# Two hybrid decoder layers in fp32r: the float32 work between the weights' matmuls put together at fewer points

## The chip, the cores and the metric

The kernel runs on one core of one Trainium2 chip. The metric is the device time of one execution in microseconds (us). The kernel before took 1279.74 us (median of three runs, 1278.59 to 1279.90).

## The reference, cut to what matters

Two layers over 256 tokens of width 1024. Each is a half-step SwiGLU, a layer norm, three token mixers on one input projection (a gated DeltaNet, a sliding-window attention with sinks, a cross-attention to 256 memory rows), a gated merge with one output projection, a layer norm, a second SwiGLU, a layer norm:

```python
def hybrid_layer(x, mem_n, ...):
    h = layer_norm(ALPHA * x + 0.5 * swiglu(x, ffn1_w_gu, ffn1_w_down), ln_g[0], ln_b[0])
    (dn_q, dn_k, dn_v, dn_b, dn_a, dn_z, sw_q, sw_k, sw_v, xa_q, gates) = split(h @ w_in)
    o_dn = deltanet_branch(dn_q, dn_k, dn_v, dn_b, dn_a, dn_z, ...)
    o_sw = sliding_window_attention(sw_q, sw_k, sw_v, swa_sinks)
    o_xa = memory_cross_attention(xa_q, mem_n, w_mem_kv)
    merged = sum(sigmoid(gates) * einsum('bsnc,ncd->bsnd', stack(o_dn, o_sw, o_xa), w_branch))
    h = layer_norm(ALPHA * h + merged @ w_out, ln_g[1], ln_b[1])
    return layer_norm(ALPHA * h + 0.5 * swiglu(h, ffn2_w_gu, ffn2_w_down), ln_g[2], ln_b[2])
```

All inputs and outputs are float32.

## The kernel before, in words

Every weight is streamed once, as 512 KB units of 128 rows by 1024 (`unit`, line 115 for its DMA). A unit is split into a rounded part `whi` (a cast on ScalarE) and the rest `wlo` (a subtraction on VectorE), both at line 121 in `split`. A product with weights is three fp32r matmuls (`mm3`, line 130: high by high, high by low, low by high). Activations that meet weights are split in the same way, into two halves of a tile such as `hT`. All other products (transposes at line 133, attention values, the DeltaNet's chunk products) are plain float32 matmuls. In the trace a float32 product of 128 columns is two rows, a transpose one.

In the mixers the order of TensorE's instructions is kept as written (`pinned`); elsewhere a scheduler orders them. `weave(work, steps)` runs the matmuls of the gates (`gates(n)`, eight steps of 12 matmuls, in two column halves of four units each) and of the branch outputs (`branch(n)`, four steps of 12), and calls the small float32 pieces after the step whose number stands in its table:

- `x_turn(tb)` transposes the cross-attention's probabilities of one block of 128 tokens (eight transposes into two PSUM tiles; ScalarE copies one out, VectorE the other). `x_values(tb)` multiplies them with the values and splits the result.
- `w_turn(0, hh)` is the same for the window attention: four transposes, one copy on ScalarE. `w_scores` and `w_values` are its scores and its values.
- `rec_v0`, `rec_s1`, `rec_r1`, `rec_v1`, `rec_qs`, `rec_o0`, `rec_o1` are the DeltaNet's recurrence over two chunks, eight matmul rows each through `heads`. `rec_r1` ends in four VectorE instructions at line 935 that make `R1`, and `rec_v1` reads `R1`. `rec_o0` is the first chunk's output; `finish` norms it, `finish_turn` transposes it.

The small pieces take their PSUM from two pools of two banks each: `at` and `sm`.

A projection that ends in a norm (`projA` with `ends`) computes token block 0, then block 1 in three column pieces: 512 columns into `acc`, and two of 256 into `at`. `Post.__call__` norms block 0 meanwhile and leaves two closures in `turns`; each is `to_T`, which transposes 512 normed columns into an `sm` bank and splits them into `hT` (a cast on ScalarE, a subtraction on VectorE). They run between the pieces of block 1. Behind the projection stands `Ffn.first`: for each token block 16 matmuls with the high half of `hT` (lines 323 and 324) and eight with its low half (line 326).

Of the kernel before, what the change touches and what calls it, by code (L numbers as in the profile page):

```python
# [38 lines left out]
def tile_trunk(ctx, tc, x, xT, mem, memT_, wst, lnp, memln, cvw, rows, cst, out):  # L39
# [30 lines left out]
    def at():  # L70
        return T(psT, [P, 512], "at")

    def sm():
        return T(psS, [P, 512], "sm")
# [54 lines left out]
    def matmul(*a, **k):  # L129
        return pe(nc.tensor.matmul(*a, **k))  # L130

    def transpose(*a):
        return pe(nc.tensor.transpose(*a))  # L133
# [43 lines left out]
    def projA(xt, w, kpu, nk, outs, tail=0, dsts=(), lead=0, after=None, behind=None, held=(), led=None, along=None, ends=()):  # L177

        def one(k, kk, hi, lo, tb, j):
            ts = slice(tb * P, (tb + 1) * P)  # L180
            n = [o.shape[-1] for o in outs[tb]]
            first = k == ((nu - tail) * kpu if tb and j and ends and len(outs[1]) > 2 else 0)
            c = kk * w + sum(n[:j])
            c = slice(c, c + n[j])
            mm3(outs[tb][j], (xt[0](k)[:, ts], xt[1](k)[:, ts]), (hi[:, c], lo[:, c]), first, k == nk - 1 or bool(ends and tb and j and k == (nu - tail) * kpu - 1))

        nu = nk // kpu
        units = {}

        def get(uu):  # L190
            if uu not in units:
                t = uu - (nu - tail)
                units[uu] = unit(kpu * w, dsts[t] if 0 <= t < len(dsts) else None, behind=behind if uu in held else None)
            return units[uu]

        def run(us, tb, js):
            for uu in us:
                for kk in range(kpu):
                    for j in js:
                        one(uu * kpu + kk, kk, *get(uu), tb, j)  # L200

        for tb in range(2):
            run(range(lead), tb, range(len(outs[tb])))
            if led:
                led(tb)
        for uu in range(lead, nu - tail):
            for tb in range(2):
                run([uu], tb, range(len(outs[tb])))
            if along and uu in along:
                along[uu](*newest)  # L210
        for uu in range(nu - tail, nu):
            get(uu)
        turns = ()
        if ends:
            after.early(outs[1].pop())
            outs[1] += ends
        for tb in range(2):
            for j in range(len(outs[tb])):
                run(range(nu - tail, nu), tb, [j])
                if j and turns:  # L220
                    turns.pop(0)()
            turns = after and after(tb, outs)

    def full_rows():
# [289 lines left out]
    def mixers(l, hT, mkT, mv_, post):  # L514
# [180 lines left out]
        def x_turn(tb):  # L695
            pT = prs[2 + tb] = T(p2, [P, 2, 4, P], "pt")
            for kb in range(2):
                ps = at().rearrange("p (h k) -> p h k", h=4)
                for h in range(4):
                    transpose(ps[:, h, :], prs[tb][:, h, kb * P:(kb + 1) * P], ident)  # L700
                (nc.vector.tensor_copy if kb else nc.scalar.copy)(pT[:, kb], ps)

        def x_values(tb):
            if not oX:
                oX.extend(T(pu, [P, 4, S], tag, F32R) for tag in ("u6", "u7"))
            ts = slice(tb * P, (tb + 1) * P)
            ps = at().rearrange("p (h k) -> p h k", h=4)
            for h in range(4):
                for kb in range(2):
                    matmul(ps[:, h, :], mv_[:, kb, h * P:(h + 1) * P], prs[2 + tb][:, kb, h, :], start=kb == 0, stop=kb == 1)  # L710
            split(oX[0][:, :, ts], oX[1][:, :, ts], ps)
# [36 lines left out]
        def w_turn(tb, hh):  # L748
            if hh == 0:
                wpT[tb] = [T(p2, [P, 2, 4, P], "pt") for _ in range(tb + 1)]  # L750
            for kb in range(tb + 1):
                ps = at().rearrange("p (h k) -> p h k", h=4)
                for h in range(4):
                    transpose(ps[:, h, :], wpr[tb, hh][:, h, kb * P:(kb + 1) * P], ident)

                (nc.vector.tensor_copy if kb else nc.scalar.copy)(wpT[tb][kb][:, :, 2 * hh:2 * hh + 2, :].rearrange("p v i q -> p i v q"), ps.rearrange("p (i v) q -> p i v q", v=2))
# [218 lines left out]
        def branch(n, o):  # L975
# [16 lines left out]

        weave(gates(0), {
            1: [lambda: x_scores(1), lambda: products(1, 0), lambda: products(1, 1), inverses],
            3: [lambda: x_turn(0)],
            4: [lambda: x_values(0)],
            5: [lambda: x_turn(1)],
            6: [lambda: x_values(1)],
            7: [lambda: w_scores(0, 0)],
            8: [lambda: w_scores(0, 1)]})  # L1000
        weave(branch(0, oX), {
            2: [lambda: w_turn(0, 0)],
            3: [lambda: w_turn(0, 1), begin_inverse],
            4: [lambda: w_scores(1, 0)]})
        weave(gates(1), {
            1: [lambda: w_values(0), double],
# [9 lines left out]
            3: [rec_s1],  # L1016
            4: [rec_r1]})
        weave(gates(2), {
            1: [rec_o0],
            2: [rec_v1, rec_qs],  # L1020
            3: [rec_o1],
            5: [lambda: finish_turn(0)],
            8: [lambda: finish_turn(1)]})
# [31 lines left out]
    ps = sm()  # L1055
# [125 lines left out]
```

## Time and profile before

| | |
|---|---|
| runs | 1278.59, 1279.74, 1279.90 us |
| profiled execution | 1280.75 us, span 1279.0 us |
| TensorE matmul | 1263.0 us busy, 99% |
| weight loads | 1073.8 us, 84% |
| VectorE | 866.5 us, 68% |
| ScalarE | 660.6 us, 52% |
| GpSimd | 210.6 us, 16% |
| chain that ended last | 89% TensorE, 4% DMA, 3% VectorE |

TensorE is called PE in the rows, its weight load PEld, VectorE DVE, ScalarE ACT, GpSimd POOL. Matmuls overlap in the pipeline, so the time that a matmul costs is the distance from its start to the next start, not its duration.

### The profile page before, as it was taken

What the parts mean: (1) busy time and instruction counts of PE and PEld (TensorE: products, weight loads), DVE (VectorE), ACT (ScalarE), POOL (GpSimd) and SP (SyncE); (2) the same over time, 40 slices, a digit from 0 to 9 for tenths busy, and PEclk for the clock granted to TensorE, in tenths of its full rate; (3) what the DMA queues carried; (4) which work ended last, traced back from release to release, by engine and by line L of the source; (5) the groups of instructions that cost most, each with busy time, mean ns of one, the idle gap of its engine ahead of it and who ended that gap; (6) DMA issues with size and microseconds to landing.
All of it is one profiled execution on the core that took longest, in us unless ns stands there. A gap on an engine that the chain in (4) does not pass through costs nothing.

```text
span 1279.0 us, 18765 instructions
## 1 busy us (share of the span) xinstructions
PE 1263.0 (99%) x6948; PEld 1073.8 (84%) x6948; DVE 866.5 (68%) x1271; ACT 660.6 (52%) x980; POOL 210.6 (16%) x365
## 2 busy tenths in 40 slices
PE   9999999999999999999999999999999999999997
PEld 6888889999878788888888888899987787888886
DVE  5788576886647776665776665759767388766655
ACT  6556444655664534444354554456656654444441
POOL 0232100002311202221012220010033102122200
PEclk9999999999999999999999999999999999999999
DMA  8988764655534728776667876556463256577762
GB/s 285 315 269 278 254 210 161 206 176 129 170 116 148 259 97 265 244 239 220 224 204 243 256 253 223 173 187 209 152 163 136 97 191 221 167 246 244 237 225 82
DMA packets 77499, 261.40 MB, mean 204 GB/s; under 512 B 11904, under 2 KB 13056, under 8 KB 77408
## 3 DMA queue, kind: packets, MB, share of 16 engines
q1 hardware_dynamic: 66320, 232.53, 55.2%
q0 software_dynamic: 11088, 27.68, 8.0%
q8 instruction: 54, 0.88, 0.3%
q14 instruction: 37, 0.30, 0.1%
HBM read 246.40 MB, written 13.76 MB: 203 GB/s over the span
## 4 chain that ended last, share of the span: by engine, by line
PE 89%; DMA 4%; DVE 3%; issue 2%; POOL 1%; ACT 1%; SPq 0%; DVEq 0%; ACTq 0%; POOLq 0%
PE acc L130 79%; PE at L130 3%; PE sm L130 3%; DMA raw<-in_wst_dram 2%; DVE wlo L121 2%; PE sm L133 1%; DMA w<-dr 1%; PE acc L323 1%; PE acc L324 1%; PE acc L326 1%; ACT whi L121 1%; PE at L133 1%; POOL t L797 1%; POOL l L788 0%; POOL t L798 0%
## 5 line engine op out<-in xcount | busy, mean ns | idle before, releaser
L121 DVE TENSOR_TENSOR wlo<-raw,whi 128x1024 fp32r<-128x1024 f32 (+2 forms) x403 | 489.3, 1222 | 282.1 <-ACT whi L121 280.2
L121 ACT CAST whi<-raw 128x1024 fp32r<-128x1024 f32 (+2 forms) x403 | 413.4, 1033 | 401.8 <-PE acc L130 321.4
L130 PE MATMUL acc<-whi,hT 128*128 128x512 f32 (+1 forms) x1824 | 563.2, 386 | 0.7 <-ACT whi L121 0.6
L130 PEld LDWEIGHTS acc<-whi,hT 128*128 128x128 f32 x1824 | 340.5, 188 | 70.3 <-ACT whi L121 3.0
L130 PE MATMUL acc<-wlo,hT 128*128 128x512 f32 (+1 forms) x912 | 350.7, 385 | 0.8 <-DVE wlo L121 0.8
L130 PE MATMUL acc<-whi,u 128*128 128x512 f32 x784 | 249.0, 392 | 0.0
L130 PEld LDWEIGHTS acc<-wlo,hT 128*128 128x128 f32 x912 | 171.6, 188 | 33.8 <-DVE wlo L121 1.7
L130 PEld LDWEIGHTS acc<-whi,u 128*128 128x128 f32 x784 | 147.3, 188 | 30.6
L130 PE MATMUL acc<-wlo,u 128*128 128x512 f32 x392 | 152.8, 390 | 0.0
L353 POOL DMA_DIRECT2D tr<-t x176 | 96.2, 553 | 304.3 <-DVE t L347 295.1
L130 PE MATMUL acc<-hT,whi 128*128 128x256 f32 x672 | 122.3, 284 | 0.0
L130 PEld LDWEIGHTS acc<-hT,whi 128*128 128x128 f32 x672 | 104.7, 192 | 0.0
L130 PE MATMUL acc<-hT,wlo 128*128 128x256 f32 x336 | 95.2, 283 | 0.0
L130 PEld LDWEIGHTS acc<-wlo,u 128*128 128x128 f32 x392 | 73.7, 188 | 14.7
L130 PEld LDWEIGHTS acc<-hT,wlo 128*128 128x128 f32 x336 | 64.4, 192 | 0.0
L354 POOL DMA_DIRECT2D pt<-tr x44 | 25.0, 568 | 194.7 <-DMA tr<-t 148.5
L344 ACT ACTIVATE t<-acc 128x256 f32<-128x256 f32 x88 | 33.5, 380 | 38.3 <-PE acc L130 38.2
L990 POOL TENSOR_TENSOR u<-u,gt 128x512 f32<-128x512 f32 x16 | 24.4, 1529 | 131.0 <-DVE gt L988 131.0
L345 DVE TENSOR_TENSOR t<-t,acc 128x256 f32<-128x256 f32 x88 | 36.7, 417 | 9.1 <-ACT t L344 4.7
L121 DVE TENSOR_TENSOR u<-pt,u 128x512 fp32r<-128x512 f32 x44 | 28.9, 657 | 11.8 <-ACT u L121 11.8
L121 DVE TENSOR_TENSOR u<-raw,u 128x1024 fp32r<-128x1024 f32 x24 | 30.9, 1290 | 7.4 <-ACT u L121 7.4
L130 PE MATMUL acc<-whi,w 128*128 128x512 f32 x96 | 31.8, 402 | 3.6 <-DVE w L121 3.5
(236 smaller groups left out, 1204.3 us busy)
## 6 DMA issues: line engine op xcount, KB each, us to landing
raw<-in_wst_dram SPq DMA_DIRECT2D x409, 512.0 KB, 4.4
tr<-t POOLq DMA_DIRECT2D x176, 64.0 KB, 3.8
pt<-tr POOLq DMA_DIRECT2D x44, 256.0 KB, 5.0
raw<-in_wst_dram SPq DMA_DIRECT2D x16, 324.0 KB, 2.9
gB<-in_lnp_dram SPq DMA_DIRECT2D x6, 512.0 KB, 5.9
bB<-in_lnp_dram SPq DMA_DIRECT2D x6, 512.0 KB, 5.9
w<-dr POOLq DMA_DIRECT2D x4, 512.0 KB, 11.5
t<-in_xT_dram SPq DMA_DIRECT2D x4, 256.0 KB, 6.1
```

Source lines behind the costliest of these rows:

```text
L121: return nc.scalar.copy(hi, src).ins, nc.vector.tensor_tensor(lo, src, hi.bitcast(F32), op=ALU.subtract).ins
L130: return pe(nc.tensor.matmul(*a, **k))
L133: return pe(nc.tensor.transpose(*a))
L323: nc.tensor.matmul(ps, hT[0][:, k, ts], hi[:, c], start=k == 0, stop=False)
L324: nc.tensor.matmul(ps, hT[0][:, k, ts], lo[:, c], start=False, stop=False)
L326: nc.tensor.matmul(ps, hT[1][:, k, ts], hi[:, c], start=False, stop=k == KD - 1)
L344: act = nc.scalar.activation(t[:, :, tb, :], g, AF.Silu).ins
L345: ins = nc.vector.tensor_tensor(t[:, :, tb, :], t[:, :, tb, :], u, op=ALU.mult).ins
L353: nc.gpsimd.dma_start(d[:, :, q].rearrange("b c x -> c b x"), z[32 * q:32 * q + 32].rearrange("c (b x) -> c b x", b=4))
L354: back = nc.gpsimd.dma_start(y, d.rearrange("b c q x -> (b c) (q x)")).ins
L797: nc.gpsimd.tensor_tensor(pr16[:, :, 0:n], ab[j // 8][:, j % 8, :, j + 1:16], y16[:, :, j:j + 1].to_broadcast([P, 8, n]), op=ALU.mult)
L990: nc.gpsimd.tensor_tensor(mg[tb][:, js], mg[tb][:, js], gt[tb][:, js], op=ALU.add)
```

## The change: what it does

In the mixers, `x_turn(0)` and `x_turn(1)` run together after step 4 of the first gates (before: steps 3 and 5), and `x_values(0)` and `x_values(1)` after step 6 (before: 4 and 6). As four PSUM tiles are then wanted at once, block 1 takes its two from `sm` in place of `at`. `w_turn(0, 0)` joins `w_turn(0, 1)` after step 3 of the first branch. `rec_o0` moves from step 1 of the third gates behind `rec_v1` and `rec_qs` after step 2. In `projA` both closures of `turns` run after block 1's last piece (before: one after each 256-column piece).

```diff
             for j in range(len(outs[tb])):
                 run(range(nu - tail, nu), tb, [j])
-                if j and turns:
-                    turns.pop(0)()
+                if j == 2:
+                    for f in turns:
+                        f()
...
-                ps = at().rearrange("p (h k) -> p h k", h=4)
+                ps = (sm if tb else at)().rearrange("p (h k) -> p h k", h=4)
...
-            3: [lambda: x_turn(0)],
-            4: [lambda: x_values(0)],
-            5: [lambda: x_turn(1)],
-            6: [lambda: x_values(1)],
+            4: [lambda: x_turn(0), lambda: x_turn(1)],
+            6: [lambda: x_values(0), lambda: x_values(1)],
...
-            2: [lambda: w_turn(0, 0)],
-            3: [lambda: w_turn(0, 1), begin_inverse],
+            3: [lambda: w_turn(0, 0), lambda: w_turn(0, 1), begin_inverse],
...
         weave(gates(2), {
-            1: [rec_o0],
-            2: [rec_v1, rec_qs],
+            2: [rec_v1, rec_qs, rec_o0],
             3: [rec_o1],
```

TensorE's order at the third gates of layer 0, before, from `rec_r1` to the first matmuls behind `rec_qs`. `sm_3931` is `rec_r1`, `sm_3963` is `rec_o0`, `sm_4008` is `rec_v1`, `sm_4015` is `rec_qs`; the `acc` rows are weights.

```order
L130 MATMUL sm_3931<-w_462_2587,u_385_2070 128x128 x4
...
L130 MATMUL acc_3943<-whi_3945,hT_1598 128x512
L130 MATMUL sm_3963<-w_461_2586,u_463_2588 128x128 x4
L130 MATMUL acc_3942<-whi_3991,hT_1598 128x512
...
L130 MATMUL acc_3943<-whi_3991,hT_1598 128x512
L130 MATMUL sm_4008<-w_462_2587,w_471_2598 128x128 x4
L130 MATMUL sm_4015<-w_462_2587,u_386_2071 128x128 x4
L130 MATMUL acc_3942<-whi_4022,hT_1598 128x512
```

The same place now; `sm_3980` is `rec_v1`, `sm_3987` is `rec_qs`, `sm_3994` is `rec_o0`.

```order
L130 MATMUL sm_3931<-w_462_2587,u_385_2070 128x128 x4
...
L130 MATMUL acc_3943<-whi_3945,hT_1598 128x512
L130 MATMUL acc_3942<-whi_3963,hT_1598 128x512
...
L130 MATMUL acc_3943<-whi_3963,hT_1598 128x512
L130 MATMUL sm_3980<-w_462_2587,w_471_2598 128x128 x4
L130 MATMUL sm_3987<-w_462_2587,u_386_2071 128x128 x4
L130 MATMUL sm_3994<-w_461_2586,u_463_2588 128x128 x4
L130 MATMUL acc_3942<-whi_4022,hT_1598 128x512
```

Between `rec_r1` and `rec_v1` there is one float32 group fewer; it stands behind `rec_qs` now.

ScalarE's order at layer 0's last norm, before. The `hT` rows are the casts of the transposed blocks: `sm_5966` and `sm_5991` are block 0's first and second 512 columns, `sm_6017` and `sm_6026` are block 1's; the `whi` rows are weights of the next SwiGLU.

```order
L279 ACTIVATE rstd_5919<-bnmv_5917,epsc 128x1
L121 CAST hT_5911<-sm_5966 128x4x128
L121 CAST whi_6052<-raw_6051 128x1024
L121 CAST whi_6124<-raw_6123 128x1024
L121 CAST hT_5911<-sm_5991 128x4x128
L279 ACTIVATE rstd_6008<-bnmv_6006,epsc 128x1
L121 CAST hT_5911<-sm_6017 128x4x128
```

The same place now (`sm_5984` is block 0's first 512 columns):

```order
L280 ACTIVATE rstd_5919<-bnmv_5917,epsc 128x1
L121 CAST whi_6052<-raw_6051 128x1024
L121 CAST whi_6124<-raw_6123 128x1024
L121 CAST hT_5911<-sm_5984 128x4x128
L121 CAST hT_5911<-sm_5991 128x4x128
L280 ACTIVATE rstd_6008<-bnmv_6006,epsc 128x1
L121 CAST hT_5911<-sm_6017 128x4x128
```

Block 0's first cast stands behind the two casts of weights now, not ahead of them.

TensorE's order at layer 0's second norm, as the difference of the two (`sm_4470`, now `sm_4488`, is block 0's first 512 columns, `sm_4495` its second; the `at` rows are block 1's last two pieces).

```order
 L130 MATMUL at_4284<-u_788_4367,w_754_4250 128x256
-L133 MATMUL sm_4470<-cs,h_218 128x128 x4
 L130 MATMUL at_4285<-u_773_4337,w_751_4247 128x256
...
 L130 MATMUL at_4285<-u_788_4367,w_754_4250 128x256
+L133 MATMUL sm_4488<-cs,h_218 128x128 x4
 L133 MATMUL sm_4495<-cs,h_218 128x128 x4
```

The first four transposes stand behind the last piece's 18 matmuls now, directly ahead of `Ffn.first`. The same holds in layer 1's second norm and in layer 0's last. At the two first norms, and where the last norm writes the output, the order of TensorE is as it was.

## Rows read from the trace of the kernel before

**Rows 1.** The page's first part: busy time and share of each engine.
```profile
PE 1263.0 (99%) x6948; PEld 1073.8 (84%) x6948; DVE 866.5 (68%) x1271; ACT 660.6 (52%) x980; POOL 210.6 (16%) x365
```

**Rows 2.** PE's longest total wait: who, for whom, us in all, times, longest.
```profile
PE acc L130 <- DVE w L121: 3.5, 4, 1.1
```

**Rows 3.** Timeline of PE around float32 groups: start us, us, instruction, count.
```profile
304.75 0.39 PE L130 MATMUL acc<-whi,hT 128*128 128x512 f32 x1
...
307.48 1.03 PE L133 MATMUL at<-cs,pp 128*128 128x128 f32 x8
...
311.11 1.95 PE L130 MATMUL at<-pt,u 128*128 128x128 f32 x16
...
315.63 1.03 PE L133 MATMUL at<-cs,pp 128*128 128x128 f32 x8
...
333.37 0.60 PE L133 MATMUL at<-cs,pp 128*128 128x128 f32 x4
...
336.56 0.60 PE L133 MATMUL at<-cs,pp 128*128 128x128 f32 x4
```

**Rows 4.** Timeline of layer 0's recurrence, `rec_r1` to `rec_qs`.
```profile
390.75 1.05 PE L130 MATMUL sm<-w,u 128*128 128x128 f32 x8
...
394.37 1.05 PE L130 MATMUL sm<-w,u 128*128 128x128 f32 x8
...
397.60 0.60 DVE L935 SCALAR_TENSOR_TENSOR w<-sm,neg,u 128x128 f32<-128x128 f32 x2
...
397.79 0.39 PE L130 MATMUL acc<-whi,hT 128*128 128x512 f32 x1
...
398.34 1.13 PE L130 MATMUL sm<-w,w 128*128 128x128 f32 x8 [0.16 <-DVE w L935]
...
399.51 0.58 ACT L942 COPY w<-sm 128x512 f32<-128x512 f32 x1 [0.24 <-PE sm L130]
...
400.12 0.48 PE L130 MATMUL acc<-whi,hT 128*128 128x512 f32 x1
```

**Rows 5.** The same `rec_v1` in layer 1.
```profile
1030.84 1.13 PE L130 MATMUL sm<-w,w 128*128 128x128 f32 x8 [0.16 <-DVE w L935]
```

**Rows 6.** Timeline of PE and ACT at layer 0's last norm.
```profile
638.40 0.40 PE L130 MATMUL at<-whi,u 128*128 128x256 f32 x2
...
638.76 2.00 ACT L121 CAST whi<-raw 128x1024 fp32r<-128x1024 f32 x2 [1.23 <-PE at L130]
...
639.23 0.48 PE L323 MATMUL acc<-whi,hT 128*128 128x512 f32 x1
...
640.67 0.58 ACT L121 CAST hT<-sm 128x512 fp32r<-128x512 f32 x1
...
641.30 0.50 PE L323 MATMUL acc<-whi,hT 128*128 128x512 f32 x1
```

**Rows 7.** Timeline of PE, ACT and DVE at layer 0's second norm.
```profile
454.55 0.60 PE L133 MATMUL sm<-cs,h 128*128 128x128 f32 x4
...
457.46 0.48 PE L323 MATMUL acc<-whi,hT 128*128 128x512 f32 x1
...
457.74 0.58 ACT L121 CAST hT<-sm 128x512 fp32r<-128x512 f32 x1 [1.97 <-PE sm L133]
...
458.40 0.64 DVE L121 TENSOR_TENSOR hT<-sm,hT 128x512 fp32r<-128x512 f32 x1
...
460.86 1.42 DVE L287 SCALAR_TENSOR_TENSOR h<-h,rstd,bB 128x512 f32<-128x512 f32 x2
...
461.76 0.63 PE L133 MATMUL sm<-cs,h 128*128 128x128 f32 x4
```

**Rows 8.** Timeline around the window's transposes and its first values.
```profile
337.19 0.59 ACT L756 COPY pt<-at 128x512 f32<-128x512 f32 x1 [1.23 <-PE at L133]
337.88 3.90 ACT L121 CAST whi<-raw 128x1024 fp32r<-128x1024 f32 x4
...
344.25 1.08 PE L130 MATMUL at<-pt,swv 128*64 128x512 f32 x4 [0.18 <-DVE pp L731]
```

## The prediction

> **What bounds the kernel now.** I read the busy times first: TensorE is busy 1263 of 1279 us [rows 1], so the time is the sum of what its instructions cost plus what it waits. Then the waits: the longest of them in total is 3.5 us in the whole run [rows 2]. So no other engine bounds the kernel over a long stretch, and a change of order can act in two ways alone: through a fixed price that each change between weights and float32 has on TensorE, or through a few short waits that it removes or makes. For the first I read the timeline of TensorE around float32 groups of different size, for the second the timelines of all engines at the moved places.
>
> **The price of a change between weights and float32.** Distances between starts tell it [rows 3]. From 304.75 to 307.48 stand 12 matmuls of weights and nothing else: 2.73 us. From 307.48 to 311.11 stand eight transposes and 12 such matmuls: 3.63. From 333.37 to 336.56 four transposes and 12: 3.19. So four transposes more cost 0.44, or 0.11 each; eight make 0.88 of the 0.90 over the plain 12, and the fixed price of a group is 0.02 us. The values say the same: 16 rows with 12 matmuls take 4.52 [rows 3], eight rows of the recurrence with 12 take 3.62 [rows 4], so 0.90 for eight rows, 0.89 left for the group of eight, and nothing fixed. Four merges a layer (`x_turn`, `x_values`, `w_turn`, `rec_o0`) make eight in all. Bounds: 0 (values) and 8 x 0.03 = 0.25 us; I take a gain of 0.15. All of this is on the path.
>
> The first weights' matmul behind such a group keeps TensorE longer than a plain one, which invites the reading that switching is dear; but the sums above hold that effect already. The Trainium skill gives a reason ("TensorE: Matmul & The Clock Gate", section "LDWEIGHTS (loading the stationary operand)"): a load takes as many nanoseconds as it has columns, divided by 1.2, which is 107 ns for 128. By that a transpose costs its weight load, wherever it stands, and putting groups together saves nothing at all; by the rows it saves the 0.15. The trace's 0.11 us a transpose agrees with the rule.
>
> **Cross-attention and window transposes.** Nothing waits at the old places, so no stall goes. At the new ones each result has a step of 12 matmuls, 2.73 us, or more before it is read; behind it are one or two copies on ScalarE or VectorE (0.59 each, as the copy in [rows 8]), which may stand behind one cast of weights (3.90 / 4 = 0.98 us [rows 8]). The sum, 2.2, fits. If that cover were gone, the price is one copy, about 0.6 us a place. I cost them at nothing, with one exception: after `w_turn`, ScalarE makes two copies in a row (the second starts about 0.1 late) before four casts of weights; VectorE's subtractions and the scores' first step follow, and `w_values(0)` at 344.25 already waits for these [rows 8]. Before, the casts began 0.10 us after the copy's end (337.19 + 0.59 = 337.78, 337.88), so 0 to 0.1 a layer; I take 0.05, and 0.1 in all.
>
> **`rec_o0`.** `rec_v1` needs `R1` from VectorE. Its last two instructions run from 397.60 to 398.20, and `rec_v1` starts at 398.34, 0.14 later; TensorE's previous matmul began at 397.79 and would have let it start at 398.02 [rows 4]. So TensorE waits 0.32 us here, and the same row with the same wait stands in layer 1 [rows 5]. Between `rec_r1` and this wait stood `rec_o0`, worth 0.89 us. Taken out, TensorE comes at 397.13. VectorE's queue up to `R1` is unchanged by the move, so `rec_v1` still starts at 398.34 and the wait is 1.21. `rec_o0` is then paid behind `rec_qs`: the weights that came at 400.12 come at 401.01. Its bank is the one that `rec_v1` filled, and ScalarE has copied that at 399.51 + 0.58 = 400.09, just in time. So +0.89 us a layer, 1.8 in all. Bounds: 0, if `R1` came that much earlier, and 1.0 a layer if that copy slips by a tenth behind a cast. I take 0.89, since all of `R1`'s chain starts from `rec_s1` and `rec_r1`, which don't move. What is late next is the norm of the first chunk on VectorE, read by `finish_turn(0)` three steps later, 8.2 us, which holds it.
>
> **Layer 0's last norm.** Here ScalarE's order decides. Before, the cast of block 0's first 512 columns ran under block 1's last piece, and the first matmul with `hT` started at 639.23 [rows 6]. Now that cast stands behind two casts of weights which wait for the slots that the last piece frees: the first began at 638.76, just after the matmul of 638.40 had ended. TensorE comes there 0.44 earlier (four transposes fewer ahead), so the casts begin at 638.32. Before, the next `hT` cast began 1.91 after them (640.67) and took 0.58: now 640.23 to 640.81. TensorE starts 0.05 after such a cast (641.30 against 640.67 + 0.58) [rows 6], so at 640.86 in place of 639.23: 1.63 late. Given back: the wait at 641.30 for the second cast (0.14: eight matmuls of 0.23 and one long one from 639.23 would have ended at 641.16), and as much again in small waits at block 1's transposes. Net 1.35; bounds 1.0 and 1.65.
>
> **The two second norms.** No cast of weights stands between. The cast of the block's second half began at 457.74; the first half's transposes stand 0.44 ahead of those of the second, so its cast runs from 457.30 to 457.88, and the first matmul moves from 457.46 to 457.93, +0.47 [rows 7]. VectorE now subtracts twice in place of once (0.64) before it goes on with block 1's norm, but begins 0.4 sooner: its output half moves from 460.86 to about 461.10. Block 1's transposes, which waited for it a tenth of a microsecond before (460.86 + 0.71, ready near 461.7), then wait for TensorE alone and come at 461.76 - 0.11 + 0.47 = 462.12. So +0.36 a norm; bounds 0.2 and 0.65; 0.7 in all.
>
> **Sum.** -0.15 + 0.1 + 1.8 + 1.35 + 0.7 = +3.8 us, against the profiled execution of 1280.75, which gives 1284.55. That execution lies 1.0 above the median of the runs, 1279.74, so the median should become 1283.5. Two medians of this kernel can be told apart from about 0.2%, 2.6 us.
>
> **Rivals.**
> - *Not slower: the moved pieces carry their own slack.* If `R1` is not held by VectorE but by TensorE's `rec_r1` in truth, it comes 0.89 earlier when TensorE does; and if ScalarE's two casts of weights find their slots free, they are done under block 1's last piece. Then only -0.15 + 0.1 + 0.7 = +0.65 is left, or -0.15 + 0.1 = -0.05 with the second norms hidden too: 1279.7 to 1280.4. For it: a cast of weights waits for a slot and data, not for the float32 work. Against it: the wait before 638.76 is put down to TensorE's matmuls, and the pair at 397.60 has other VectorE work ahead. It decides where `rec_v1`'s wait stays at 0.3.
> - *Half of it comes back.* The recurrence's or the last norm's delay is absorbed by a later wait for weights or for the merge's transposes. Without the one or the other the sum is 2.0 or 2.4: 1281.7 to 1282.2. For it: the waits of [rows 2] are of that kind. Against it: these waits hang on TensorE's own earlier results, so they move along.
> - *More: PSUM.* Four banks are full of probabilities or values at once; a score piece finds `at` not yet emptied, because ScalarE's splits stand behind a cast that waits for its slot. One cast and one copy, 0.98 + 0.59 = 1.6 us a layer: 1286.7. For it: ScalarE's casts wait for TensorE at nearly every step. Against: the count above fits.
>
> **Chances.** The forecast 0.62, the first rival 0.12, the second 0.18, the third 0.08. The range that holds eight in ten leaves out the first and the third: from 1280.8, below the second rival, to 1285.8, above the forecast with all upper bounds (1.0 a layer, 1.65, 0.65 a norm, 0.1 a layer, no gain: 5.2 over the median, 1284.9) and the runs' own scatter of 1. Slower by over 0.2%: the forecast, less a few hundredths for its lower end, and the third rival, 0.67; within: the first two and that lower end, less 0.05, which I leave to faster for a saving that no row shows: 0.28.
>
> **What will show it.** `rec_v1`'s wait for VectorE of 0.16 should read about 1.05 in both layers, with `R1`'s last pair ending as long after `rec_r1` as before. At layer 0's last norm TensorE's first matmul on `hT` should wait about 1.6 us for ScalarE, behind two casts of weights; in the second norms about 0.5. The groups of 16 transposes should take twice those of eight. The prediction is wrong if the distance from step to step in the gates falls by more than 0.05 us a merge, or if the wait before `rec_v1` has not grown.

## The result and the profile after

The changed kernel took 1285.11 us (median of eight runs, 1282.55 to 1290.50), the kernel before 1278.42 beside it (eight runs, 1277.78 to 1280.38): a ratio of 1.0049, 95% interval 1.0033 to 1.0064. It is slower, by 6.7 us where 3.8 were forecast. Two executions among all that follow, one of the kernel before (7219.72 us) and one of `e8_best` (1795.30), lie far outside the others and are left out of every range and ratio.

The profiled execution took 1285.91 us. First its busy times and PE's waits (who, for whom: us in total, times, longest):

```profile
PE 1263.7 (98%) x6948; PEld 1074.5 (84%) x6948; DVE 866.8 (67%) x1271; ACT 660.8 (51%) x980; POOL 210.4 (16%) x365
```

```profile
PE acc L130 <- DVE w L121: 3.4, 4, 1.1
PE sm L130 <- DVE w L936: 2.2, 2, 1.1
PE acc L130 <- ACT whi L121: 1.9, 1, 1.9
PE acc L324 <- ACT hT L121: 1.9, 3, 1.4
```

The work is the same (1263.0 us in [rows 1]); the span is 1284.1 instead of 1279.0. PE's old longest wait stands as it did [rows 2]; the second line (`rec_v1` for `R1`) has grown from 0.3 us, the fourth (the norms' first matmuls for their casts) is new, and the third, at the start of the program, which the change doesn't touch, has grown from 0.6.

How much later the same weights' matmul starts than before, place by place, gives this account:

| place | us |
|---|---|
| start of the program, up to 24 us | +1.7 |
| cross-attention's groups, two layers | -0.05 each |
| `w_turn`, two layers | -0.03 each |
| wait at `w_values(0)`, layers 0 and 1 | 0.0 and -0.2 |
| `rec_o0`, layers 0 and 1 | +0.93, +0.91 |
| second norm, layers 0 and 1 | +0.42, +0.38 |
| layer 0's last norm | +1.42, 0.25 of it given back |
| all | +5.1, of which 3.45 behind the start |

The recurrence in layer 0, on PE, DVE and ACT:

```profile
392.35 1.05 PE L130 MATMUL sm<-w,u 128*128 128x128 f32 x8
...
399.20 0.60 DVE L936 SCALAR_TENSOR_TENSOR w<-sm,neg,u 128x128 f32<-128x128 f32 x2
399.95 1.13 PE L130 MATMUL sm<-w,w 128*128 128x128 f32 x8 [1.09 <-DVE w L936]
...
400.91 2.00 PE L130 MATMUL sm<-w,u 128*128 128x128 f32 x16
401.11 0.58 ACT L943 COPY w<-sm 128x512 f32<-128x512 f32 x1 [1.05 <-PE sm L130]
...
402.67 0.48 PE L130 MATMUL acc<-whi,hT 128*128 128x512 f32 x1
```

From `rec_r1`'s start to the end of `R1`'s last pair it is 399.80 - 392.35 = 7.45 us, as it was (398.20 - 390.75 in [rows 4]). `rec_v1` waits 1.09 for it instead of 0.16. The 16 rows behind it are `rec_qs` and `rec_o0`.

Layer 0's last norm on PE and ACT, and below it the second norm:

```profile
640.93 0.40 PE L130 MATMUL at<-whi,u 128*128 128x256 f32 x2
...
641.29 1.99 ACT L121 CAST whi<-raw 128x1024 fp32r<-128x1024 f32 x2 [6.09 <-PE at L130]
...
641.40 1.03 PE L133 MATMUL sm<-cs,h 128*128 128x128 f32 x8
...
643.19 1.06 ACT L121 CAST hT<-sm 128x512 fp32r<-128x512 f32 x2
...
643.82 0.50 PE L324 MATMUL acc<-whi,hT 128*128 128x512 f32 x1 [1.39 <-ACT hT L121]
```

```profile
459.21 1.04 PE L133 MATMUL sm<-cs,h 128*128 128x128 f32 x8
...
459.85 1.08 ACT L121 CAST hT<-sm 128x512 fp32r<-128x512 f32 x2 [6.89 <-PE sm L133]
...
460.49 0.50 PE L324 MATMUL acc<-whi,hT 128*128 128x512 f32 x1 [0.24 <-ACT hT L121]
...
464.72 0.60 PE L133 MATMUL sm<-cs,h 128*128 128x128 f32 x4
```

In the last norm the two casts of weights stand in front of the two of `hT`, and PE waits out all of them. In the second norm none does, and only 0.24 us is left to wait (layer 1 shows the same 0.24).

The merged groups, with the weights' matmul behind each:

```profile
311.89 1.03 PE L133 MATMUL at<-cs,pp 128*128 128x128 f32 x8
312.76 1.04 PE L133 MATMUL sm<-cs,pp 128*128 128x128 f32 x8
313.55 0.48 PE L130 MATMUL acc<-whi,hT 128*128 128x512 f32 x1
...
319.11 3.73 PE L130 MATMUL at<-pt,u 128*128 128x128 f32 x32
...
322.60 0.48 PE L130 MATMUL acc<-whi,hT 128*128 128x512 f32 x1
```

Sixteen transposes keep the weights away for 313.55 - 311.89 = 1.66 us, 0.10 each, and 32 rows of values for 3.49, 0.11 each, as groups of half the size did [rows 3]. There is next to no fixed price to save.

The start of the program: PE's first rows with a wait, and the window around them (us; busy us of PE, PEld, DVE, ACT, POOL with instructions; granted clock of TensorE; DMA share; GB/s):

```profile
10.43 0.73 PE L130 MATMUL acc<-whi,hT 128*128 128x512 f32 x2 [1.89 <-ACT whi L121]
11.69 0.79 PE L130 MATMUL acc<-wlo,hT 128*128 128x512 f32 x1 [0.52 <-DVE wlo L121]
```

```profile
10.00:15.00 5.00, 4.05 (x10) 2.93 (x11) 4.22 (x5) 3.51 (x5) 0.00 (x0) 0.66 1.02 400
```

Behind the two waits the granted clock is 0.66 on average over the window, that is, partly on its 1.2 GHz level. In the trace of before PE stood there for 0.65 and 0.53 us, and the same window has 1.00. PE waits for ACT, and ACT for a DMA: its cast of a part of the input, before and after, is

```profile
7.83 0.62 ACT L121 CAST hT<-t 128x512 fp32r<-128x512 f32 x1 [0.50 <-DMA t<-in_xT_dram]
```

```profile
8.04 0.62 ACT L121 CAST hT<-t 128x512 fp32r<-128x512 f32 x1 [1.72 <-DMA t<-in_xT_dram]
```

Up to the first norm, 185 us into the program, all fourteen traces have the same instructions in the same order on every engine. Still six have a stretch at the 1.2 GHz level there (this one, `e1_norms`, `e5_after_again`, `e6_after_inv`, `e7_xw_inv`, `e11_casts`; PE's longest wait for ACT there is 1.00 to 1.94 us in them) and eight have none (0.3 to 0.98 us). `e7_xw_inv` and `e8_best` are the same program up to layer 0's third gates, and one has it and the other not. Five of the six have the change of the norms in them, and of the eight only `e12_after_pp`; as the instructions are the same, no row says how that could act.

### The profile page after: what moved, and what is told of

The parts are those of the page before. It is cut to its first block, busy times and chain, and to the rows that moved or that the text cites. A ratio compares the mean times of both kernels' runs of the same rounds, so it can differ in the third digit from the quotient of the medians.

```text
span 1284.1 us, 18771 instructions
## 1 busy us (share of the span) xinstructions
PE 1263.7 (98%) x6948; PEld 1074.5 (84%) x6948; DVE 866.8 (67%) x1271; ACT 660.8 (51%) x980; POOL 210.4 (16%) x365
## 4 chain that ended last, share of the span: by engine, by line
PE 92%; DMA 3%; DVE 3%; ACT 1%; issue 1%; SPq 0%; DVEq 0%; ACTq 0%
PE acc L130 81%; PE at L130 4%; PE sm L130 3%; DMA raw<-in_wst_dram 3%; DVE wlo L121 1%; PE sm L133 1%; PE acc L324 1%; PE acc L327 1%; PE acc L325 1%; ACT whi L121 1%; PE at L133 1%; DVE u L121 0%; DVE w L121 0%; ACT u L121 0%; ACT hT L121 0%
## 5 line engine op out<-in xcount | busy, mean ns | idle before, releaser
L346 DVE TENSOR_TENSOR t<-t,acc 128x256 f32<-128x256 f32 x88 | 36.6, 416 | 11.1 <-ACT t L345 7.5
```

What stands on the lines that cost most here:

```text
L346: ins = nc.vector.tensor_tensor(t[:, :, tb, :], t[:, :, tb, :], u, op=ALU.mult).ins
```

## The experiments

The theory: the rows behind the merges are right, nothing is saved, and the order costs 3.5 us (`rec_o0` behind `R1`'s chain, the norms' casts behind others). Rivals: the merges themselves cost something; or the excess over 3.5 us has a cause of its own. Twelve runs of eleven new kernels and the changed one, on three chips, each beside the kernel before.

### e1_norms: the norms alone

```diff
-                if j and turns:
-                    turns.pop(0)()
+                if j == 2:
+                    for f in turns:
+                        f()
```

> Only the norms' part of the change (both of block 0's transposes behind block 1's last piece), the rest as before. Theory (waits): in the trace, TensorE's first matmul on hT waits 1.39 us for ScalarE at layer 0's last norm and 0.24 in each second norm, and the program loses 1.35 + 2 x 0.36 = 2.1 us against before between the start-up and the end; no wait of 1.1 us before rec_v1. Rival (the timed runs lose more than the profile shows, because every new wait also costs clock or start-up time in the same proportion, 6.7 us of medians for 3.45 us of trace): 4 us. Rival (the part is harmless, rec_o0 alone decides): 0.

Measured: 1280.73 us (11 runs, 1280.08 to 1285.46), ratio to before 1.0009 (0.9999 to 1.0019); the lowest run lies 2.1 above before's lowest, the medians 1.0 apart. The interval, from about nothing to 2.4 us, holds the expected 2.1 and nearly the rival's 0, and leaves out the 4; between the first two the trace decides. PE's waits for ACT `hT` are those of the changed kernel (1.9 in three places, the longest 1.38), the steps +0.42, +2.41 and +0.37. The profiled run was the slowest of its eleven, and shows why the middle one, the last norm, cost 2.41 and not 1.17: ahead of it DVE waited 1.62 us for the norm's offset `bB` to arrive by DMA, and block 1's transposes then 0.67 for DVE. That load is not part of the change; there was no wait for it in the traces of before and of the changed kernel, one of 1.31 in `e3_xw`, which keeps the old norms, and one of 1.88 in `e6_after_inv`.

### e2_o0: `rec_o0` alone

```diff
-            1: [rec_o0],
-            2: [rec_v1, rec_qs],
+            2: [rec_v1, rec_qs, rec_o0],
```

> Only rec_o0 moved behind rec_qs, the rest as before. Theory (waits): the wait before rec_v1 reads 1.05 to 1.1 us in both layers, and the program loses 2 x 0.89 = 1.8 us. Rival (cost in proportion to the waits in timed runs): 3.5 us. Rival (R1 follows TensorE, so the wait stays at 0.16): 0.

Measured: 1282.45 us (11 runs, 1281.10 to 1284.79), ratio 1.0020 (1.0012 to 1.0029). Wait before `rec_v1` 2.2 us in two places, steps +0.94 and +0.94. Behind them 0.53 and 0.33 are gone again where the branches are merged: PE waits there for DVE `w` before and after. The move need not be the cause: this wait is 3.5 us in all in the trace of before [rows 2] and 1.5 to 3.4 in the thirteen others, and in `e3_xw`, which leaves `rec_o0` in its place, 0.31 and 0.95 are gone there.

### e3_xw: the attentions' merges alone

```diff
-                ps = at().rearrange("p (h k) -> p h k", h=4)
+                ps = (sm if tb else at)().rearrange("p (h k) -> p h k", h=4)
...
+            4: [lambda: x_turn(0), lambda: x_turn(1)],
+            6: [lambda: x_values(0), lambda: x_values(1)],
...
+            3: [lambda: w_turn(0, 0), lambda: w_turn(0, 1), begin_inverse],
```

> Only x_turn, x_values and w_turn put together, the norms and rec_o0 as before. Theory (a group has a fixed price of 0.02 us or less): -0.05 us a layer at the cross-attention, -0.03 at w_turn, in all -0.15 to -0.3 us; no verdict in the times. Rival (a change between weights and float32 has a price of its own of about 0.09 us, the longer distance behind a group): -0.5 us or more. Rival (PSUM or ScalarE late): slower by 0.5 us or more.

Measured: 1281.36 us (12 runs, 1279.24 to 1285.35), ratio 1.0014 (1.0004 to 1.0024). The steps at the merged places are -0.05 and -0.03, as in the theory. What is over came in this trace at layer 0's last norm (1.2 us, behind the late `bB`) and, the larger part, in layer 1 at `w_values(0)`. There PE's row before was

```profile
976.75 1.08 PE L130 MATMUL at<-pt,swv 128*64 128x512 f32 x4 [0.34 <-DVE pp L731]
```

Now DVE and PE there, then the window behind:

```profile
972.61 0.45 DVE L892 STREAM_TRANSPOSE w<-w 128x256 f32<-128x256 f32 x1 [5.59 <-POOL w L799]
972.98 4.59 DVE L121 TENSOR_TENSOR wlo<-raw,whi 128x1024 fp32r<-128x1024 f32 x4
977.48 1.28 DVE L731 SCALAR_TENSOR_TENSOR pp<-at,cs 128x512 f32<-128x512 f32 x2
```

```profile
978.22 1.08 PE L130 MATMUL at<-pt,swv 128*64 128x512 f32 x4 [1.70 <-DVE pp L731]
979.23 2.01 PE L130 MATMUL sm<-w,l 32*32 32x32 f32 x64
```

```profile
980.00:985.00 5.00, 5.00 (x48) 4.16 (x45) 2.07 (x6) 1.83 (x7) 0.00 (x0) 0.50 0.76 271
```

`begin_inverse` starts the last part of the inverse that the DeltaNet needs, with a stream transpose on DVE. It stands there ahead of the four subtractions that make `wlo` (some of the expectations call them weight casts) and of the scores' `pp`. It waits for GpSimd's chain (line 799), whose first operation waited 13.01 us in this trace for a round trip through DRAM; where that arrives late, `pp` is late, and PE stands 1.70 us. Behind that wait PE ran at its 1.2 GHz level (0.50 in the window; before has 1.00 there), and the place cost 4.3 us in all.

### e4_o0_first: the merge the other way round

`e3_xw`, and `rec_o0` merged in front of `rec_v1`:

```diff
-            1: [rec_o0],
-            2: [rec_v1, rec_qs],
+            2: [rec_o0, rec_v1, rec_qs],
```

> As the kernel with x_turn, x_values and w_turn put together, and rec_o0 after step 2 too, but ahead of rec_v1. Theory (the cost of rec_o0's move is that it left the place where VectorE's R1 was being made, not the merging): the wait before rec_v1 stays at 0.16 us, and the program is 0.2 to 0.4 us shorter than before. Rival (three float32 pieces at one place are what costs, through the two sm banks): 0.9 us a layer longer, as with rec_o0 behind.

Measured: 1280.33 us (11 runs, 1278.32 to 1285.84), ratio 1.0011 (1.0000 to 1.0023); 2.1 below `e2_o0` on the same chip, though the attentions' merges are in it. The row of `rec_v1` in layer 0 has no wait left:

```profile
396.91 1.05 PE L130 MATMUL sm<-w,u 128*128 128x128 f32 x8
...
398.06 1.16 PE L130 MATMUL sm<-w,w 128*128 128x128 f32 x8
```

So the merge as such costs nothing; that `rec_o0` no longer covers `R1`'s chain does. The time is not the 0.2 to 0.4 us below before that were expected, but 0.6 above: the early `begin_inverse` is in it, and PE waited 0.60 and 1.07 at `w_values(0)`.

### e5_after_again: the changed kernel once more

> The changed kernel once more, unaltered, beside the kernel before and the three variants that follow it. The steps that the trace shows beside the weights' matmuls add up to 3.45 us (0.90 + 0.91 for rec_o0, about 1.4 for layer 0's last norm, 0.4 to 0.5 and 0.38 for the second norms, less 0.05 and 0.03 for the merges of each layer); the medians of its first runs stood 6.7 us above before. Theory A: the change costs those 3.5 us in every execution, and what is over comes in some executions alone, from the wait of PE before w_values(0) that ended 0.18 to 1.70 us late in six traces and from the stretches of PE at the 1.2 GHz level behind a wait; then the lowest of the runs lie 3 to 4.5 us above the lowest of before, and the median 5 to 7 us above its median. Rival B: a part of the change that the steps do not show costs 3 us in every execution; then the lowest runs too lie 6 us or more above before's lowest.

Measured, on a second chip: 1290.78 us (five runs, 1287.60 to 1291.33), ratio 1.0077 (1.0062 to 1.0092), 11.2 above before's median and 9.6 above its lowest run. By the bounds set ahead that is the rival's side. The trace shows no new step, though: `rec_o0` and the second norms have those of the first trace within 0.1 us, the last norm 1.58 (`bB` was 1.90 late for DVE), the start 1.5, and layer 1's `w_values(0)` waited 1.57 us with the 1.2 GHz level behind it, 4.2 together. Outside its stretches at the 1.2 GHz level this execution has a granted clock of 0.95 from 5 us to its end, where the other traces have 1.00; no time is lost by it, as the weights' matmuls start 0.227 us apart as they do elsewhere.

With the early `begin_inverse` there are sixteen such places in eight traces. Where the last of the round trip's data had landed up to 16.4 us after its write (line 781) was issued, PE waited 0.17 to 0.60 us at `w_values(0)`; at 16.6 it waited 0.34 and 1.04, at 16.8 1.07, at 18.1 and 18.2 1.57 and 1.70. So the wait follows the DMA.

### e6_after_inv: the changed kernel, the inverse begun behind `pp`

```diff
-            with tc.issue_after(wpr["end"]):
+            with tc.issue_after(wpr["pp"]):
...
-            4: [lambda: w_scores(1, 0)]})
+            4: [lambda: w_scores(1, 0), begin_inverse]})
```

> The changed kernel, with begin_inverse issued one place later on DVE: its stream transpose stands behind both scores' pp instead of ahead of them, so that GpSimd's late chain no longer holds pp, for which PE's w_values(0) waits. Theory A (the over-long executions come through that wait): no wait of PE at w_values(0) above 0.35 us in either layer, the norms' waits on the hT casts (1.4, 0.24) and the wait before rec_v1 (1.1) as in the changed kernel, median 1 to 3 us below the changed kernel's in the same runs, 3 to 4.5 us above before, and few runs with a lower clock. Rival B (the scatter has another source, the start-up's loads for one): w_values(0) waits nothing, and yet median and scatter are the changed kernel's, 5 to 7 us above before. Rival C: the inverse itself, begun later, is late for its reader; a wait of 0.5 us or more appears before rec_v1 or products of the inverse.

Measured, beside the run above: 1284.66 us (six runs, 1283.75 to 1289.52), ratio 1.0042 (1.0026 to 1.0057), 6.1 below the unaltered changed kernel. One instruction's place on DVE is worth that much, so on this chip most of the 7.7 us over the steps' 3.5 came through `w_values(0)`. But PE still waited there, 0.78 and 0.75, and the median is 5.1 above before, not 3 to 4.5. The next run shows why it still waits; in the rest of its trace PE waits 1.9 at the start and 1.34 at the last norm, where DVE waited for `bB`.

### e7_xw_inv: the same edit with the attentions' merges alone

Norms and `rec_o0` as before, the edit of `e6_after_inv`.

> The kernel before with the merges of the cross-attention and of w_turn alone (norms and rec_o0 as before), and begin_inverse behind the scores' pp as in the run ahead of this. With the early begin_inverse these merges gave 1.0014 in 12 runs, though the steps in the trace were 0.05 and 0.03 us shorter in each layer. Theory A (the wait at w_values(0) made the difference): median 0.2 to 0.6 us below before, its runs as close together as before's (clock 0.997 or more in all but one or two). Rival B (the merged float32 stretches themselves lower the granted clock in some executions): w_values(0) waits nothing, a third of the runs still shows a clock of 0.994 or 0.995, median 1 to 2 us above before.

Measured: 1280.24 us (12 runs, 1278.49 to 1282.26), ratio 1.0003 (0.9994 to 1.0011). Neither the expected gain of 0.2 to 0.6 nor the loss of `e3_xw` shows. GpSimd's line 799 in layer 0, before and here, then DVE and PE here:

```profile
336.94 0.74 POOL L799 TENSOR_TENSOR w<-t,cs 128x256 f32<-128x256 f32 x1
```

```profile
340.23 1.59 POOL L799 TENSOR_TENSOR w<-t,cs 128x256 f32<-128x256 f32 x1
```

```profile
339.98 5.19 DVE L121 TENSOR_TENSOR wlo<-raw,whi 128x1024 fp32r<-128x1024 f32 x4 [4.29 <-ACT whi L121]
345.09 1.28 DVE L731 SCALAR_TENSOR_TENSOR pp<-at,cs 128x512 f32<-128x512 f32 x2
```

```profile
345.83 1.08 PE L130 MATMUL at<-pt,swv 128*64 128x512 f32 x4 [0.75 <-DVE pp L731]
```

DVE now runs beside GpSimd's last operations instead of after them. The four subtractions take 5.19 us where they took 4.59 alone (`e3_xw`), GpSimd's line 799 takes 1.59 against 0.74, and PE waits the difference. The Trainium skill ("SBUF — State Buffer", section "Who interferes with whom") says that an elementwise operation of VectorE with both inputs in SBUF contends with GpSimd's reads; the trace agrees, by 0.6 us for DVE and 0.85 for GpSimd.

### e8_best: and `rec_v1` one stretch later

```diff
             1: [rec_o0],
-            2: [rec_v1, rec_qs],
-            3: [rec_o1],
+            3: [rec_v1, rec_qs],
+            4: [rec_o1],
```

> The run ahead of this, and rec_v1 with rec_qs one stretch later (behind rec_o0 by two stretches of the weights' matmuls, rec_o1 one later too), so that the pair's hand-over from rec_o0 to rec_v1 lies under other matmuls: before, PE stands there for 0.16 to 0.32 us in each layer. Theory A: no wait before rec_v1, 0.3 us less in each layer, so 0.6 us below the run ahead of this and 0.8 to 1.2 us below before. Rival B: rec_v1 was not short of its operand but its followers are; rec_o1 or finish_turn then wait for DVE or ACT by as much, and the time is that of the run ahead of this.

Measured: 1279.85 us (ten runs, 1278.26 to 1282.99), ratio 1.0004 (0.9995 to 1.0014). The wait before `rec_v1` is gone in both layers and the steps are -0.43 and -0.41, a little more than expected, but the time is that of `e7_xw_inv` within its noise. In layer 0 the trace loses 0.72 again where the branches are merged: PE waits 0.66 us for ACT `w` and, 1.8 us later, 1.10 for DVE `w`, and a stretch at the 1.2 GHz level follows (0.78 and 0.88 in the windows from 430 to 440 us). Whether the pieces behind take the gain back in every execution (rival B) one trace can't tell.

### e9_pp: `pp` ahead of two weight casts

```diff
-                wpr["pp"] = nc.vector.scalar_tensor_tensor(...)
+                with tc.high_priority(offset=2 * AHEAD) if (tb, hh) == (1, 0) else nullcontext():
+                    wpr["pp"] = nc.vector.scalar_tensor_tensor(...)
```

> The run e8_best, and in both layers the two pp of w_scores(1, 0) ahead of two of the four weight casts on DVE that stood in front of them. In the two runs with a late begin_inverse PE still waited 0.75 to 0.78 us at w_values(0) wherever GpSimd's chain ended late: the four casts wlo in front of pp took 5.2 us beside GpSimd against 4.6 in the kernel before. Theory A: with two casts between, pp ends some 2.5 us earlier and PE does not wait at w_values(0) at all; the matmuls behind need the two later casts no sooner, so each layer is 0.2 to 0.8 us shorter than in e8_best, the median 0.5 to 1.2 us below before and no run above before's range comes from that place. Rival B: the wait goes over to the weights' matmuls behind w_values(0), which then stand for DVE wlo by 0.5 us or more; the median is that of e8_best, within 0.3 us of before. Rival C: the scatter is the start-up's; median as e8_best, and the runs lie as far apart.

Measured, on a third chip: 1288.43 us (five runs, 1286.61 to 1290.53), ratio 1.0068 (1.0053 to 1.0083). All three expectations missed. `w_values(0)` waits nothing, but on DVE three of the four subtractions and part of the scores' softmax now stand ahead of the stream transpose, and the doubling behind `w_values(0)` reads what it writes (the wait is put down to the small `sk` right behind it). DVE and PE in layer 0, and the window behind:

```profile
346.65 0.43 DVE L893 STREAM_TRANSPOSE w<-w 128x256 f32<-128x256 f32 x1
```

```profile
343.21 1.08 PE L130 MATMUL at<-pt,swv 128*64 128x512 f32 x4
347.14 1.51 PE L130 MATMUL sm<-w,l 32*32 32x32 f32 x64 [2.85 <-DVE sk L740]
```

```profile
348.00:353.00 5.00, 5.00 (x43) 4.06 (x40) 0.34 (x2) 3.29 (x12) 0.00 (x0) 0.66 0.35 138
```

PE waits 2.85 us there, 2.47 in layer 1, and the granted clock falls behind it in both layers, to 0.66 in this window; every one of the five runs has a mean clock of 0.996 or less.

### e10_gap: the kernel before with a longer wait at `w_values(0)`

```diff
-                nc.vector.transpose(W[:, 512:768], W[:, 768:1024])
+                for _ in range(7):
+                    nc.vector.transpose(W[:, 512:768], W[:, 768:1024])
```

> The kernel before with nothing moved; begin_inverse's stream transpose (0.45 us) is issued seven times instead of once (it writes the same values again), so that DVE gets to pp later: by about 1.4 us in layer 0, where DVE had 0.8 us to spare, and 2.2 us in layer 1 (0.36 us for each repeat). PE's waits at w_values(0) become about 1.6 us (from 0.18) and 2.5 us (from 0.34). Theory A: a wait of that length is followed by some 6.8 us of PE at the 1.2 GHz level, as in the two traces where it was 1.57 and 1.70 us, so each layer costs its wait and 2.5 to 3 us more: steps of 4 to 5 us at both places, together +8 to +10 us, in every run. Rival B: the low clock comes by chance and not from the wait; then the steps are 1.4 and 2.2 us, the time +3.6 us, and the clock stays at 0.998.

Measured: 1289.27 us (seven runs, 1282.45 to 1294.44), ratio 1.0073 (1.0047 to 1.0098). The profiled run is one of the two quick ones, 1282.71:

```profile
979.68 1.08 PE L130 MATMUL at<-pt,swv 128*64 128x512 f32 x4 [2.32 <-DVE pp L731]
980.69 1.51 PE L130 MATMUL sm<-w,l 32*32 32x32 f32 x64
```

Its waits are 1.85 and 2.32 us, its steps +1.66 and +1.95, and the granted clock stays at 1.00: the 64 small matmuls take 1.51 us, not the 2.01 of `e3_xw`. The other five runs took 1286.85 to 1294.44 with a mean clock of 0.991 to 0.995, where 12 runs of before beside them have one of 0.996 and none lower. So both expectations were too simple: such a wait does not lower the clock each time, but in five of seven runs, and then the time is 4 to 12 us longer.

### e11_casts: `e1_norms` with the norms' casts earlier on ACT

```diff
-        split(hi[:, :, ts], lo[:, :, ts], ps.rearrange("p (j t) -> p j t", j=4))
+        with tc.high_priority(offset=2 * AHEAD) if early else nullcontext():
+            split(hi[:, :, ts], lo[:, :, ts], ps.rearrange("p (j t) -> p j t", j=4))
```

> The norms' change alone, with the casts of each norm's first block put on ACT by a higher priority: at layer 0's last norm one weight cast instead of two stands ahead of the hT casts. Theory A (the 1.39 us wait of PE for ACT hT there is the two weight casts in front, 1.99 us, less what PE still had to do): the wait falls by one cast, 0.95 us, to about 0.45 us, and the step at that place from 1.36 to about 0.4 us; the second norms, which had no weight cast in front, keep their 0.24. Rival B: the hT casts themselves (1.06 us behind the transposes) are the wait; it stays above 1 us.

Measured: one run, 1281.81 us. Layer 0's last norm:

```profile
639.58 1.05 ACT L121 CAST whi<-raw 128x1024 fp32r<-128x1024 f32 x1 [6.08 <-PE at L130]
...
640.53 1.06 ACT L121 CAST hT<-sm 128x512 fp32r<-128x512 f32 x2
...
641.16 0.50 PE L325 MATMUL acc<-whi,hT 128*128 128x512 f32 x1 [0.44 <-ACT hT L121]
```

One cast of weights fewer in front takes the wait from 1.38 to 0.44 and the net step to 0.43, from 1.17 in the changed kernel (2.41 in `e1_norms`, with its late `bB`). The wait was ACT's queue.

### e12_after_pp: the changed kernel with the edits of e6_after_inv and e9_pp

> The changed kernel with both edits at w_values(0): the stream transpose behind pp, and pp ahead of two weight casts. All of the change is in it. Theory A (of the changed kernel's excess, 3.5 us are the rows of the norms and of rec_o0, and the rest comes through w_values(0), the low clock behind it and the start-up): no wait at w_values(0), the steps 0.9 + 0.9 for rec_o0, 1.4, 0.5 and 0.4 for the norms as before, median 3 to 4.5 us above before in the same runs (2.5 to 3.5 us above e9_pp). Rival B (the change costs more than its steps in every run): median 5 us or more above before although w_values(0) does not wait.

Measured: 1292.16 us (four runs, 1291.38 to 1294.42), ratio 1.0100 (1.0084 to 1.0115). As in `e9_pp` PE waits behind `w_values(0)`, 2.46 and 3.02 us, so the distance to before (12.2 us) decides between neither expectation. Against `e9_pp`, which differs by the norms and by the places of `rec_o0`, `rec_v1`, `rec_qs` and `rec_o1` alone, it is 3.7 us in the medians and 4.6 in the spans; the steps of the norms and of `rec_o0` in its own trace come to 3.8, and `e9_pp` gains 0.43 in each layer at `rec_v1`: 4.6 together, the distance of the spans.

## Why the prediction was right or wrong

- *The fixed price of a group* (-0.15): right. The merges of `x_turn`, `x_values` and `w_turn` measured -0.08 in each layer, -0.16 in all, and 16 or 32 rows cost what they cost apart.
- *`w_turn`* (+0.1): wrong in sign, by little. `w_values(0)` waited 0.19 in both layers, against 0.18 and 0.34. The extra copy on ACT did not lengthen it. What lengthens it, in seven of the sixteen places with the early `begin_inverse`, is the late end of GpSimd's chain, which the step did not look at; in the other nine it is 0.17 to 0.19.
- *`rec_o0`* (+0.89 a layer): right, 0.93 and 0.91. `R1` ended as long after `rec_r1` as before, and the bank was free in time. `e4_o0_first` shows the cause.
- *The norms' first matmuls*: the mechanism and the delays were right; PE's waits themselves were 1.39 and 0.24, where about 1.6 and 0.5 were named. In the trace of before the transposes ahead of them in the last and in the second norm are these:

```profile
638.87 0.60 PE L133 MATMUL sm<-cs,h 128*128 128x128 f32 x4
```

```profile
457.10 0.60 PE L133 MATMUL sm<-cs,h 128*128 128x128 f32 x4
```

- *Layer 0's last norm*: the first `hT` matmul followed them by 0.36 us [rows 6] and now follows the first of eight by 2.42; four more take 0.44, so it is 1.62 late (1.63 forecast). Given back were 0.45 instead of 0.28, so it nets 1.17 and not 1.35.
- *The second norms* (+0.36 each): 0.42 and 0.38. In layer 0 the first matmul followed by 0.36 [rows 7], now by 1.28: 0.48 late, as forecast (0.47), and 0.06 of it was given back instead of 0.11.
- *The sum*: 3.8 forecast for the change, 3.45 in the trace behind its start, and between the medians of `e12_after_pp` and `e9_pp` 3.7, of which 0.9 are a gain of `e9_pp` that is no part of the change. The medians moved by 6.7, and 1285.11 lies inside the range of 1280.8 to 1285.8. That is in part luck: the forecast counted from 1279.74, and the kernel before took 1278.42 beside the changed one; on the second chip the changed kernel took 1290.78, outside. What the forecast left out is in its last step, adding the account of one execution to the median of the runs. It took every wait that the change leaves in place as constant. Three of them hang on a DMA whose arrival varies: the start (+1.7 here), `w_values(0)` (0.17 to 1.70 in the traces) and `bB` (0 to 1.9 us on DVE), and behind a long one the clock may fall. A fourth, PE's wait for DVE `w` in the merges, was longer in the trace of before (3.5 us) than in any other, so that the distance of the two traces, too, is that of two executions.
- *The rivals*: in the trace neither the pieces' own slack nor a later wait took the cost back (the lag of 2.53 us behind layer 0's recurrence is 2.54 ahead of the second norm, that of 4.86 in layer 1 is 4.76), and no bank of PSUM came late.

The three parts alone (`e1_norms`, `e2_o0`, `e3_xw`) cost 1.0, 2.7 and 1.7 us in the medians, 5.4 together, where the steps in the changed kernel's trace are 2.0, 1.8 and -0.2. The 1.7 of the merges is not a price of merging: with the late `begin_inverse` (`e7_xw_inv`) it is gone within the noise. That `w_values(0)` carries the larger part of the excess is shown by `e6_after_inv` on its chip.

Two things stay open. Why do the merges make the long wait there likelier? With the early `begin_inverse`, nine of 36 runs with the attentions' merges have a mean clock of 0.996 or less and three of 92 without; with the late one (`e6_after_inv`, `e7_xw_inv`, `e8_best`), three of 28, one of them (0.948, in 1282.26 us) perhaps of the harmless kind of `e5_after_again`. The rows give a candidate. SyncE issues these weight loads around the moment when the round trip's read-back is issued (layer 0, us from that moment):

| load | first | second | third | fourth | fifth |
|---|---|---|---|---|---|
| before | -4.4 | -1.9 | 1.3 | 6.2 | 9.5 |
| after | -4.4 | -2.3 | 0.8 | 4.9 | 7.6 |

The fourth stands at 6.1 to 6.4 in both layers of all five traces without the merges and at 4.7 to 5.0 in all nine with them, so more weights are asked for while the read-back is under way. The read-back took 11.1 to 12.8 us in the ten places without the merges and 11.5 to 16.4 in the eighteen with them, over 13 in eight. That the earlier loads delay it is not shown: no run moves them alone. And why was the excess 6.7 us in the first runs and 11.2 on the second chip? Traces of single executions can't tell how often each wait was long.

No version beat the kernel before: the best, `e8_best` and `e7_xw_inv`, are equal to it.

## What to carry to other kernels

Before merging work of another kind on a saturated engine, measure the fixed price of one group by the distances between starts; at 0.02 us there is nothing to win, and the small piece that is moved away was covering someone's chain or keeping a cast ahead in a queue. Look for in-order waits on a DMA with a variable arrival (here DVE's stream transpose) that stand ahead of what the saturated engine reads: one profiled execution shows them as short as they happened to be. Where the profiled engine's wait grows to a microsecond or two, look at the granted clock behind it before adding up waits.

## What the runs showed of the hardware

- A wait of PE of 1.57 and 1.70 us was followed by the 1.2 GHz level in two traces (`e5_after_again`, `e3_xw`), one of 1.85 and one of 2.32 in a third were not (`e10_gap`), and one of 2.85 was again (`e9_pp`), as were two of 0.66 and 1.10 that began less than 2 us apart (`e8_best`). Which it is varies from execution to execution: of the seven runs of `e10_gap` five have a mean clock of 0.991 to 0.995 and two 0.998.
- One execution had a granted clock of 0.95 nearly throughout, and its matmuls of weights still started 0.227 us apart (`e5_after_again`).
- The same round trip through DRAM took between 14.9 us (`e2_o0`, layer 0) and 20.3 us (`e12_after_pp`, layer 1) from the issue of its write to the last landing of its read-back (28 places in 14 traces).
- DVE's four subtractions of 128x1024 took 4.6 us alone (`e3_xw`) and 5.2 beside GpSimd (`e7_xw_inv`), whose 128x256 operation took 1.6 instead of 0.74.
